# Wider-spaced modulated tiles, and thirteen modulation vectors made in another place, in a four-layer diffusion step

## The chip, the cores and the metric

The kernel runs on one core of a Trainium2 chip. The metric is the device time of one execution in microseconds. Its engines are named as in the profile: PE (TensorE, matmuls), DVE (VectorE), ACT (ScalarE), POOL (GpSimd) and SP (SyncE, which here only issues DMAs).

## What is computed

One step of a network of four layers over 384 tokens of 1024 channels: 128 context tokens and 256 latent tokens. Every layer is a mixer and an MLP, each on a normalised and modulated copy of the residual stream:

```python
for i in range(DEPTH):                       # 4 layers: recurrent, conformer, attention, recurrent
    sh1, sc1, g1, sh2, sc2, g2 = _adaln(cond, w_mod[i], b_mod[i])   # silu(cond) @ w + b, in 6 parts
    h = _rmsnorm(x) * (1 + sc1) + sh1
    x = x + g1 * mixer(h)
    h = _rmsnorm(x) * (1 + sc2) + sh2
    x = x + g2 * (jnp.square(jax.nn.relu(h @ w1)) @ w2)             # 1024 -> 4096 -> 1024
```

All of it is in fp32. The mixers are a bidirectional gated linear recurrence (layers 0 and 3), a gated convolution of width 31 (layer 1), and neighbourhood attention over a grid (layer 2).

## The kernel before

**Products.** Channels lie on the 128 partitions, tokens in the free dimension, so the stream x is eight tiles of 128 x 384. An fp32 product is made of three matmuls in a faster 32-bit format (`mm3`): both operands are split into a rounded part and the rest, and PE adds up hi x hi, hi x lo and lo x hi. Weights come in chunks of 1 MB ("raw", two buffers, on SP's queue); ACT writes the rounded part (whi, L212) and DVE the rest (wlo, L213), five buffers of 128 x 1024 each, so that weights are split well ahead of their use. All matmuls are issued at L125; the profile tells them apart by their output's name: rec, gbr, lo (recurrent layer), pw, cps (conformer), qk, v, s, pt, wo (attention), f and o (MLP). An MLP runs in two halves; in each, eight f products make 16 hidden tiles of 128 x 384 (hh and hl), and eight o products of 48 matmuls each bring them back to the residual tiles.

**The modulated copy.** `htile` (L397) gives the moving operands of f, qk, pw, rec and gbr: eight pairs of tiles, hhi and hlo, of 128 x 386, 384 tokens and two columns for the shift. The first 96 matmuls of a layer or MLP after the first stream all 386 columns of a copy not yet normalised (`Norm.start`), and the norm is applied to their result; the rest stream the 384 columns of the normalised one. Before the norm is known PE issues 24 of them, then the matmuls of the norm's total (n_1p, at `MID`). The norm's sum (n_1s) is closed on DVE after the last residual.

**Modulation vectors.** There are 4 x 6 x 8 = 192 of them, each made from 512 KB of weights, in a fixed order. `pe_mod` makes them on PE in batches of two or more (loads pmw or pmwl; 32 small matmuls into pmp for two vectors, then two matmuls with `sel` and an addition on DVE, L292). `dve_mod` (L312) makes one on DVE: a load dmw on SP's queue, two passes over it (mjunk, L325, 128 x 1024) and an addition (L328). Where each is made is written down by hand: calls `mods(n)` in the recurrent layer (PE), a call in the conformer with buffers of its own ("pm", two of them), one entry of `ATTMODS` for each pair of heads in attention, and `MLPMODS`, a number after each of the eight f or o products of a half. `need` makes at once what a layer asks for and is not there.

**Around the conformer's convolution.** Six of the eight channel tiles are convolved on PE (cps): POOL writes the padded tile to memory (zd) and reads it back in shifted windows (z, four loads), SP loads the diagonal weights (dg). Later, SP loads pmwl2 to pmwl5 for six vectors that are made on PE while PE would stand idle; two of them use the "pm" buffers, which the call `dve_mod(2, cp)` has used before, and two the z buffers.

**Order.** A scheduler places each engine's instructions by its own costs, within what buffers and dependences allow; an engine then works through its list in order, and so does SP with its loads.

Of the kernel before, what the change touches and what calls it, by code (L numbers as in the profile page):

```python
# [8 lines left out]
F32R = mybir.dt.float32r  # L9
# [5 lines left out]
P = 128  # L15
D = 1024
KT = D // P
DEPTH = 4
SEQ = 128
LAT = 256  # L20
N = SEQ + LAT
# [16 lines left out]
GW = 64  # L38
WR = 8
WC = 16  # L40

SH1, SC1, G1, SH2, SC2, G2 = range(6)

# [17 lines left out]
def weight_plan():  # L61
    plan = []
    for l in range(DEPTH):
# [11 lines left out]
        for half in range(2):  # L75
# [14 lines left out]
WARM0, WARM1, WARM2 = 20, 8, 4  # L90
RECLAG, PRE1 = 2, 8
WARM3 = (6, 6)
MLPMODS = {(False, 0, 1): (0, 1, 2, 1, 2, 1, 2, 1), (False, 0, 2): (2, 2, 2, 1, 2, 2, 2, 1),
           (False, 1, 1): (2, 2, 2, 1, 2, 2, 2, 1), (False, 1, 2): (0, 0, 0, 0, 0, 0, 0, 0),
           (True, 0, 1): (0, 1, 1, 1, 1, 2, 2, 0), (True, 0, 2): (0,) * 8,
           (True, 1, 1): (0,) * 8, (True, 1, 2): (0,) * 8}
ATTMODS = (0, 1, 1, 1, 1, 1, 1, 1)
VALMODS = 0
PTB, BTB = 3, 3
NMOD = DEPTH * 6 * KT  # L100
# [13 lines left out]
def trunk(ctx, tc, wst, wmod, vecs, condr, xin, kcT, vcache, rpbt, diag, ident_in,  # L114
          y_out, st_out, k_out, v_out):
    nc = tc.nc
# [3 lines left out]
    act = ctx.enter_context(tc.tile_pool(name="act", bufs=1))  # L120
# [14 lines left out]
    def tmp(name, dt=F32):  # L135
        return tp.tile([P, 400], dt, tag="t", name=name, bufs=7)
# [86 lines left out]
    def chunk(*key):  # L223
        i = state["w"]
        assert plan[i] == key, (plan[i], key)
        state["w"] = i + 1
        ensure(i + 2)
        return loaded[i]
# [3 lines left out]
    def mod_tile(l):  # L232
        if l not in modv:
            modv[l] = cst.tile([P, 6, KT, 2], F32, name=f"modv{l}")
        return modv[l]
# [6 lines left out]
    def next_mod(form):  # L242
        i = len(MODS)
        if i >= NMOD:
            return None
        MODS.append((form,) + order[i])
        return i, order[i]
# [64 lines left out]
    def dve_mod(n, pool=None):  # L312
        for _ in range(n):
            nx = next_mod("dve")
            if nx is None:
                return
            i, (l, m, c) = nx
            if pool:
                w = pool.tile([P, D], F32, tag="pm", name=f"dmw{i}", bufs=2)
            else:  # L320
                w = wp.tile([P, D], F32, tag="dmw", name=f"dmw{i}", bufs=3)
            nc.sync.dma_start(w, wmod[i])
            for s in range(2):
                tc.keep_in_program_order(
                    nc.vector.scalar_tensor_tensor(mjunk, w, 0.5, condb[:, s], op0=ALU.mult, op1=ALU.mult,  # L325
                                                   accum_out=mod_tile(l)[:, c, m, s:s + 1]))
            dst = mod_tile(l)[:, c, m, :]
            nc.vector.tensor_tensor(dst, dst, bmod[:, l, c, m, :], op=ALU.add)  # L328
# [66 lines left out]
            return r  # L395

    def htile(name):  # L397
        return (act.tile([P, N + 2], F32R, tag="hhi", name=name + "h", bufs=KT),
                act.tile([P, N + 2], F32R, tag="hlo", name=name + "l", bufs=KT))

    def split(src, hi, lo):
        nc.scalar.activation(hi, src, AF.Copy)
# [174 lines left out]
    def lru(l, j, nrm):  # L577
        with tc.tile_pool(name=f"lru{l}", bufs=1) as lp:
# [9 lines left out]
            def conv(b, i, ps, c=None):  # L588
                t = 2 * b + i
                r = recs[t % 2]  # L590
                for s, xa, xb in SEG:
                    o = 1 + 2 * s
                    if c is None:
                        nc.scalar.activation(r[:, xa + o:xb + o], ps[:, xa:xb], AF.Copy)
                    else:
                        nc.scalar.activation(r[:, xa + o:xb + o], ps[:, xa:xb], AF.Identity, bias=c[:, s:s + 1])
                if b not in xfs:
                    xfs[b] = lp.tile([P, 2, LG], F32, tag="xf", name=f"xf{l}{b}", bufs=2)
                xf = xfs[b][:, i]
                nc.vector.tensor_scalar(xf, r[:, 0:LG], lcw[:, j, t, 0:1], lcb[:, j, t:t + 1],  # L600
                                        op0=ALU.mult, op1=ALU.add)
                for k in range(1, 4):
                    nc.vector.scalar_tensor_tensor(xf, r[:, k:k + LG], lcw[:, j, t, k:k + 1], xf,  # L603
                                                   op0=ALU.mult, op1=ALU.add)
# [67 lines left out]
            def outs(b):  # L672
                if b < 3:
                    w_ = lp.tile([P, 1024], F32R, tag="graw", name=f"yh{l}{b}", bufs=3)
                else:
                    w_ = lp.tile([P, 4 * LG], F32R, tag="a", name=f"yh{l}{b}")
                if b:
                    lo = lp.tile([P, 2, N], F32R, tag="gl", name=f"yl{l}{b}", bufs=4)
                else:
                    lo = lp.tile([P, 2, LG], F32R, tag="xf", name=f"yl{l}{b}", bufs=2)[:, :, :N]  # L680
                for i in range(2):
                    y.append(split(gls[b][:, i], w_[:, i * N:i * N + N], lo[:, i]))

            def mods(n, pe=0):
                if l == 0:
                    dve_mod(n)
                    pe_mod(pe)

            y = []
            if l == 0:  # L690
                h = []
# [36 lines left out]
            else:  # L728
                h = nrm.start([chunk("rec", j, b) for b in range(2)], f"rec{l}_0_",
                              lambda i, t, c: conv(i // 2, i % 2, t, c))  # L730
            gbr(0)
            mods(1)
            q = gates(0)
# [21 lines left out]
            gbr(3)  # L755
            combine(3, q3)
            outs(3)
            mods(0, 4)
            nc.sync.dma_start(st_out[j], nst)
            mv = need(l, G1)  # L760
            nc.vector.tensor_scalar_mul(mv[:, G1], mv[:, G1], 0.5)
            return out_proj(l, "lout", j, y, f"lo{l}")

    def mlp(l, nrm):
        last = l == DEPTH - 1
        with tc.tile_pool(name=f"mlp{l}", bufs=1) as mp:
            for half in range(2):
                hid = []

                def act_(i, ps, c=None):  # L770
                    r = tmp(f"r{l}{half}{len(hid)}")[:, :N]
                    s = tmp(f"s{l}{half}{len(hid)}")[:, :N]
                    hh = mp.tile([P, N], F32R, tag="hh", name=f"hh{l}{half}{len(hid)}", bufs=16)
                    hl = mp.tile([P, N], F32R, tag="hl", name=f"hl{l}{half}{len(hid)}", bufs=16)
                    if c is None:
                        nc.scalar.activation(r, ps[:, :N], AF.Relu)  # L776
                    else:
                        for s_, a, b in SEG:
                            nc.scalar.activation(r[:, a:b], ps[:, a:b], AF.Relu, bias=c[:, s_:s_ + 1])
                    nc.scalar.activation(hh, r, AF.Square)  # L780
                    nc.scalar.activation(s, r, AF.Square)  # L781
                    nc.vector.tensor_tensor(hl, s, hh.bitcast(F32), op=ALU.subtract)  # L782
                    hid.append((hh, hl))

                i = 0
                while i < 8:
                    if half == 0 and i == 0:
                        h = nrm.start([chunk("ff1", l, 0), chunk("ff1", l, 1)], f"f{l}0_", act_)
                        i = 2
                    else:  # L790
                        lin([chunk("ff1", l, half * 8 + i)], h, f"f{l}{half}{i}_", act_)
                        i += 1
                    dve_mod(MLPMODS[last, half, 1][i - 1])
                mv = need(l, G2)
                if half == 1:
                    nx = Norm(l + 1, SC1, SH1)
                for m in range(KT):
                    hi, lo = chunk("ff2", l, half * 8 + m)
                    ps = mm_tile(f"o{l}{half}{m}")[:, :N]
                    for k in range(16):  # L800
                        o = (k % 8) * P
                        mm3(ps, hi[k // 8][:, o:o + P], lo[k // 8][:, o:o + P], hid[k], k == 0, k == 15)
                    residual(m, ps, G2, mv)
                    if half == 1:
                        nx.add(m)
                    dve_mod(MLPMODS[last, half, 2][m])
        return nx

    hb1 = cst.tile([P, 2 * KT], F32, name="hb1")
# [8 lines left out]
    def conformer(l, j, nrm):  # L818
        mv = need(l, G1)
        with (tc.tile_pool(name=f"cf{l}", bufs=1) as cp,  # L820
# [93 lines left out]
            def shift():  # L914
# [3 lines left out]
                for m in first:  # L918
# [3 lines left out]
            h = nrm.start([chunk("pw1", j, m) for m in range(2)], f"pw{l}0_",  # L922
                          lambda i, t, c: keep.__setitem__(i, (t, c)))
# [14 lines left out]
            conv_pe(3)  # L938
            pwin(6)
            pwin(7)  # L940
            dve_mod(2, cp)
            conv_pe(4)
            shift()
            conv_pe(5)
# [18 lines left out]
            m = KT - 1  # L963
# [62 lines left out]
    def attention(l, j, nrm):  # L1026
        with tc.tile_pool(name=f"na{l}", bufs=1) as ap:
# [184 lines left out]
            both(values(0), None)  # L1212
            dve_mod(ATTMODS[0])
            both(attend(0), values(1))
            for pr in range(1, KT):
                dve_mod(ATTMODS[pr])
                both(attend(pr), qk(pr + 1) if pr + 1 < KT else wo_first())
# [25 lines left out]
def lay_out(i):  # L1243
# [75 lines left out]
    for cq in range(GW):  # L1319
        c0 = min(max(cq - WC // 2, 0), GW - WC)  # L1320
        for rq in range(4):
            bt[:, rq, cq, :, c0:c0 + WC] = rpb[:, WR - 1 - rq:WR + 3 - rq, c0 - cq + WC - 1:c0 - cq + 2 * WC - 1]
    bt = bt.reshape(NH, 2, P, LAT)
# [46 lines left out]
```

## Time and profile before

| | |
|---|---|
| median of 3 runs | 1767.76 us (1767.61 to 1771.6) |
| profiled execution | 1769.54 us, span 1767.8 us, mean granted clock of PE 0.994 |
| layer 0 with its MLP | to 460.8 us |
| layer 1 with its MLP | to 887.3 us |
| layer 2 with its MLP | to 1340.9 us |
| layer 3 with its MLP, final norm | to the end |
| modulation vectors | 42 on PE, 150 on DVE |

In the lines below, a row of groups has line, engine, operation, out<-in, shape and count, then busy time in us and mean ns of one, then the engine's idle time ahead of them and what ended it. A row of the chain has start, length and work. A row of the windows has for each engine its busy time, then PE's granted clock, the share of time that the DMA engines were busy, and GB/s. A row of waits has the waiting line, what it waited for, us in total, times, and the longest.

### The profile page before, as it was taken

Reading aid. Unit: us, or ns where it says so; the run is one execution under the profiler, and the core shown is the slowest. Engines: PE = TensorE matmul, PEld = TensorE weight load, DVE = VectorE, ACT = ScalarE, POOL = GpSimd, SP = SyncE. Lnnn points to the kernel's source line nnn. Section 1 sums busy time; section 2 is a strip of 40 time slices with the busy share of each in tenths; the row PEclk is TensorE's granted clock in tenths of the full one; section 3 lists DMA queues with packets and bytes.
Section 4 is the critical chain, followed back from the end, with each engine's and each line's share of the span. In section 5 each row is a group of like instructions: output and inputs, shape, how many; then the busy total and the mean of one; then the engine's idle time right before and its main releaser. Section 6 shows DMA issues by size and latency. Waiting matters only on the chain.

```text
span 1767.8 us, 27418 instructions
## 1 busy us (share of the span) xinstructions
PE 1733.9 (98%) x10510; PEld 1633.5 (92%) x10510; DVE 1394.3 (79%) x2773; ACT 943.9 (53%) x1699; POOL 21.6 (1%) x46
## 2 busy tenths in 40 slices
PE   8999999999998999999999999999999999999997
PEld 7778999999984999999987889999999789999997
DVE  5998999895787889988576778998998979953443
ACT  4876662453632774255355556624545976733531
POOL 0000000000021000000000000000000000000000
PEclk9999999999999999999999999999999999999999
DMA  9666467674376247766345534676664413543341
GB/s 387 233 215 214 136 229 243 239 240 141 122 229 193 63 153 260 242 237 226 120 173 171 168 109 143 227 250 238 230 242 136 134 70 120 202 143 119 119 136 44
DMA packets 66996, 322.43 MB, mean 182 GB/s; under 512 B 7952, under 2 KB 12176, under 8 KB 43696
## 3 DMA queue, kind: packets, MB, share of 16 engines
q1 hardware_dynamic: 64944, 314.11, 51.5%
q0 software_dynamic: 1920, 6.57, 1.5%
q8 instruction: 82, 1.34, 0.3%
q14 instruction: 50, 0.41, 0.1%
HBM read 316.69 MB, written 3.96 MB: 181 GB/s over the span
## 4 chain that ended last, share of the span: by engine, by line
PE 85%; DVE 9%; ACT 4%; DMA 2%; issue 1%; POOL 0%; SPq 0%; DVEq 0%; ACTq 0%
PE f L125 30%; PE o L125 30%; PE pw L125 4%; PE qk L125 4%; PE lo L125 3%; PE p L125 2%; PE wo L125 2%; PE v L125 2%; PE cps L125 2%; PE rec L125 2%; DVE wlo L213 1%; DVE mjunk L325 1%; PE po L125 1%; DVE xf L603 1%; DVE tr L645 1%
## 5 line engine op out<-in xcount | busy, mean ns | idle before, releaser
L212 ACT ACTIVATE whi<-raw 128x1024 fp32r<-128x1024 f32 x360 | 378.3, 1058 | 553.6 <-PE o L125 333.1
L213 DVE TENSOR_TENSOR wlo<-raw,whi 128x1024 fp32r<-128x1024 f32 x360 | 438.1, 1222 | 170.3 <-ACT whi L212 169.9
L325 DVE SCALAR_TENSOR_TENSOR mjunk<-dmw,condb 128x1024 bf16<-128x1024 f32 x300 | 365.8, 1219 | 1.3
L125 PE MATMUL o<-hl,whi 128*128 128x384 f32 x1024 | 343.0, 335 | 0.0
L125 PE MATMUL o<-hh,wlo 128*128 128x384 f32 x1024 | 343.0, 335 | 0.0
L125 PE MATMUL o<-hh,whi 128*128 128x384 f32 x1024 | 343.0, 335 | 0.0
L125 PEld LDWEIGHTS o<-hh,whi 128*128 128x128 f32 x1024 | 192.2, 188 | 0.0
L125 PEld LDWEIGHTS o<-hh,wlo 128*128 128x128 f32 x1024 | 192.2, 188 | 0.0
L125 PEld LDWEIGHTS o<-hl,whi 128*128 128x128 f32 x1024 | 192.2, 188 | 0.0
L496 DVE SCALAR_TENSOR_TENSOR x<-o,modv,x 128x128 f32<-128x128 f32 (+1 forms) x128 | 47.5, 413 | 87.3 <-PE o L125 87.3
L125 PE MATMUL g<-xf,graw 128*128 128x386 f32 x256 | 85.7, 490 | 1.6 <-DVE gl L661 1.6
L782 DVE TENSOR_TENSOR hl<-s,hh 128x384 fp32r<-128x384 f32 x128 | 71.1, 556 | 11.1 <-ACT s L781 6.6
L125 PEld LDWEIGHTS g<-xf,graw 128*128 128x128 f32 x256 | 47.9, 189 | 34.2 <-DVE gl L661 2.2
L780 ACT ACTIVATE hh<-r 128x384 fp32r<-128x384 f32 x128 | 67.1, 524 | 3.4
L781 ACT ACTIVATE s<-r 128x384 f32<-128x384 f32 x128 | 65.1, 509 | 0.0
L776 ACT ACTIVATE r<-f 128x384 f32<-128x384 f32 x112 | 53.2, 475 | 10.8 <-PE f L125 10.8
L125 PE MATMUL lo<-yh,wlo 128*128 128x384 f32 x128 | 43.4, 339 | 1.3 <-DVE wlo L213 1.3
L125 PE MATMUL lo<-yh,whi 128*128 128x384 f32 x128 | 43.3, 340 | 0.0
L125 PE MATMUL cps<-z,dg 128*32 128x399 f32 (+2 forms) x448 | 34.8, 466 | 8.5 <-DMA z<-zd 8.5
L125 PE MATMUL lo<-yl,whi 128*128 128x384 f32 x128 | 43.0, 336 | 0.0
L125 PEld LDWEIGHTS cps<-z,dg 128*32 128x32 f32 x448 | 14.4, 114 | 28.1 <-issue 23.9
L892 DVE SCALAR_TENSOR_TENSOR zt<-zp,vec,zt 128x399 f32<-128x399 f32 x58 | 36.6, 632 | 1.2
(1521 smaller groups left out, 4043.9 us busy)
## 6 DMA issues: line engine op xcount, KB each, us to landing
raw<-wst SPq DMA_DIRECT2D x180, 1024.0 KB, 5.0
dmw<-wmod SPq DMA_DIRECT2D x150, 512.0 KB, 4.1
pmw<-wmod SPq DMA_DIRECT2D x38, 512.0 KB, 6.2
graw<-wst SPq DMA_DIRECT2D x16, 512.0 KB, 5.5
bt<-rpbt SPq DMA_DIRECT2D x16, 384.0 KB, 3.9
z<-zd POOLq DMA_DIRECT2D x24, 213.5 KB, 7.5
dg<-diag SPq DMA_DIRECT2D x6, 512.0 KB, 5.0
pmwl<-wmod SPq DMA_DIRECT2D x4, 512.0 KB, 6.9
```

Of the source, the lines that this page charges most:

```text
L125: i = nc.tensor.matmul(*a, **kw)
L212: nc.scalar.activation(hi, raw[:, s], AF.Copy)
L213: nc.vector.tensor_tensor(lo, raw[:, s], hi.bitcast(F32), op=ALU.subtract)
L325: nc.vector.scalar_tensor_tensor(mjunk, w, 0.5, condb[:, s], op0=ALU.mult, op1=ALU.mult, accum_out=mod_tile(l)[:, c, m, s:s + 1]))
L496: nc.vector.scalar_tensor_tensor(x[m][:, xa:xb], ps[:, a:b], mv[:, g, m, s:s + 1], x[m][:, xa:xb], op0=ALU.mult, op1=ALU.add)
L603: nc.vector.scalar_tensor_tensor(xf, r[:, k:k + LG], lcw[:, j, t, k:k + 1], xf, op0=ALU.mult, op1=ALU.add)
L645: nc.vector.tensor_tensor_scan(tr[:, 2 + mt, ::-1], a[:, 2 + mt, ::-1], ti[:, 2 + mt, ::-1], h0v[:, j, 1, t:t + 1], op0=ALU.mult, op1=ALU.add)
L776: nc.scalar.activation(r, ps[:, :N], AF.Relu)
L780: nc.scalar.activation(hh, r, AF.Square)
L781: nc.scalar.activation(s, r, AF.Square)
L782: nc.vector.tensor_tensor(hl, s, hh.bitcast(F32), op=ALU.subtract)
L892: nc.vector.scalar_tensor_tensor(t, z[:, k:k + CG], dww[:, m, k:k + 1], t, op0=ALU.mult, op1=ALU.add)
```

## The change

Three things change. (1) h tiles are allocated 512 columns wide and cut to 386, so they lie 2048 bytes apart; their tags are now hh and hl of the same pool. In the built programs they were 1568 bytes apart before, at changing offsets within 512 bytes, and all begin at the same offset after. The hidden tiles are 1536 bytes, as they were. The room comes from the descriptor scratch of POOL's DMAs, halved to 8192 bytes. (2) Four vectors on PE at the end of layer 0, two on DVE in the conformer and seven on DVE in attention are no longer made there. (3) The table for the MLPs is by layer and half: for layer 0 eleven vectors after the second half's o products, for layer 1 eight of them there and eight instead of ten after its first f products, for layer 2 seven instead of ten after its first f products and fourteen after its second half's o products. There, eleven were made before already: ten that layer 3 would ask for had been placed that early by the scheduler. Layer 3's MLP is left with four of its eight. In all 38 vectors are made on PE and 154 on DVE.

```diff
+HP = 512
-MLPMODS = {(False, 0, 1): (0, 1, 2, 1, 2, 1, 2, 1), (False, 0, 2): (2, 2, 2, 1, 2, 2, 2, 1),
-           (False, 1, 1): (2, 2, 2, 1, 2, 2, 2, 1), (False, 1, 2): (0, 0, 0, 0, 0, 0, 0, 0),
...
-ATTMODS = (0, 1, 1, 1, 1, 1, 1, 1)
+LIGHT, HEAVY, NONE = (0, 1, 2, 1, 2, 1, 2, 1), (2, 2, 2, 1, 2, 2, 2, 1), (0,) * 8
+EVEN = (1,) * 8
+MLPMODS = {0: (LIGHT, HEAVY, HEAVY, (2, 1, 2, 1, 2, 1, 2, 0)),
+           1: ((0, 1, 1, 1, 2, 1, 2, 0), HEAVY, HEAVY, EVEN),
+           2: (EVEN, HEAVY, HEAVY, HEAVY),
+           3: ((0, 1, 1, 1, 1, 2, 2, 0), NONE, NONE, NONE)}
+ATTMODS = (0,) * 8
...
     def htile(name):
-        return (act.tile([P, N + 2], F32R, tag="hhi", name=name + "h", bufs=KT),
-                act.tile([P, N + 2], F32R, tag="hlo", name=name + "l", bufs=KT))
+        return tuple(act.tile([P, HP], F32R, tag=f"h{q}", name=name + q, bufs=KT)[:, :N + 2] for q in "hl")
...
             outs(3)
-            mods(0, 4)
...
-                    dve_mod(MLPMODS[last, half, 1][i - 1])
+                    dve_mod(MLPMODS[l][2 * half][i - 1])
...
-                    dve_mod(MLPMODS[last, half, 2][m])
+                    dve_mod(MLPMODS[l][2 * half + 1][m])
...
             pwin(7)
-            dve_mod(2, cp)
             conv_pe(4)
...
-    nc = bacc.Bacc("TRN2", target_bir_lowering=False, num_devices=1)
+    nc = bacc.Bacc("TRN2", target_bir_lowering=False, num_devices=1, dynamic_dma_scratch_size=8192)
```

The change moves rows on three engines at the places that matter below. PE at the end of layer 0, before (pmp: vectors; lo: the output product, whi12 and wlo12 its first chunk, whi13 and wlo13 the next):

```order
600 L125 MATMUL lo000_1724<-yh01_1435,wlo12_0_1579 128x384
601 L125 MATMUL pmp42_1675<-pmw42_1676,condp_99 32x128 x2
602 L125 MATMUL lo001_1725<-yh01_1435,whi12_1_1582 128x384
603 L125 MATMUL lo001_1725<-yl01_1436,whi12_1_1582 128x384
604 L125 MATMUL lo001_1725<-yh01_1435,wlo12_1_1583 128x384
605 L125 MATMUL lo002_1726<-yh00_1429,whi13_0_1706 128x384
606 L125 MATMUL lo002_1726<-yl00_1430,whi13_0_1706 128x384
607 L125 MATMUL lo002_1726<-yh00_1429,wlo13_0_1707 128x384
608 L125 MATMUL lo003_1727<-yh00_1429,whi13_1_1710 128x384
609 L125 MATMUL lo003_1727<-yl00_1430,whi13_1_1710 128x384
610 L125 MATMUL pmp42_1675<-pmw43_1678,condp_99 32x128 x2
```

and after:

```order
592 L129 MATMUL lo001_1675<-yh01_1435,whi12_1_1582 128x384
593 L129 MATMUL lo001_1675<-yl01_1436,whi12_1_1582 128x384
594 L129 MATMUL lo001_1675<-yh01_1435,wlo12_1_1583 128x384
595 L129 MATMUL lo002_1676<-yh00_1429,whi13_0_1656 128x384
596 L129 MATMUL lo002_1676<-yl00_1430,whi13_0_1656 128x384
597 L129 MATMUL lo003_1677<-yh00_1429,whi13_1_1660 128x384
598 L129 MATMUL lo002_1676<-yh00_1429,wlo13_0_1657 128x384
599 L129 MATMUL lo003_1677<-yl00_1430,whi13_1_1660 128x384
600 L129 MATMUL lo002_1676<-yh00_1429,whi13_0_1656 128x384
```

The pmp rows are gone, and chunk 13 comes 24 rows after the last gbr; its wlo is asked for in row 598.

SP's queue in the conformer, before (raw: weights; dg: diagonals; pmwl: the late vectors' weights):

```order
166 L206 DMA raw58_5937<-wst 128x2048
167 L206 DMA raw59_6099<-wst 128x2048
168 L161 DMA pmwl2_5666<-wmod 128x1024
169 L854 DMA dg17_5487<-diag 128x1024
170 L161 DMA pmwl3_5668<-wmod 128x1024
171 L161 DMA pmwl4_5670<-wmod 128x1024
172 L322 DMA dmw90_6534<-wmod 128x1024
173 L161 DMA pmwl5_5672<-wmod 128x1024
```

and after:

```order
163 L165 DMA pmwl2_5661<-wmod 128x1024
164 L165 DMA pmwl3_5663<-wmod 128x1024
165 L210 DMA raw52_5013<-wst 128x2048
166 L210 DMA raw53_5088<-wst 128x2048
167 L210 DMA raw54_5163<-wst 128x2048
168 L210 DMA raw55_5344<-wst 128x2048
169 L210 DMA raw56_5419<-wst 128x2048
170 L210 DMA raw57_5922<-wst 128x2048
...
174 L210 DMA raw59_6094<-wst 128x2048
175 L855 DMA dg17_5492<-diag 128x1024
176 L165 DMA pmwl4_5665<-wmod 128x1024
177 L326 DMA dmw95_6529<-wmod 128x1024
```

pmwl2 and pmwl3 have moved ahead of raw52; behind raw59 only dg17, pmwl4 and a dmw are left.

DVE at the end of layer 2, before (x7: the last residual; n3_1s: the sum for layer 3's norm; dmw: a vector's weights):

```order
1913 L213 TENSOR_TENSOR wlo141_1_13569<-raw141_13562,whi141_1_13568 128x1024
1914 L496 SCALAR_TENSOR_TENSOR x7_86<-o217_13486,modv2_6870,x7_86 128x128
1915 L496 SCALAR_TENSOR_TENSOR x7_86<-o217_13486,modv2_6870,x7_86 128x256
1916 L213 TENSOR_TENSOR wlo142_0_13575<-raw142_13572,whi142_0_13574 128x1024
1917 L372 TENSOR_TENSOR n3_1s_13539<-n3_1a_13106,n3_1q7_13537 128x384
```

and after:

```order
1922 L217 TENSOR_TENSOR wlo141_0_13605<-raw141_13602,whi141_0_13604 128x1024
1923 L332 TENSOR_TENSOR modv3_11621<-modv3_11621,vec_70 128x2
1924 L329 SCALAR_TENSOR_TENSOR mjunk_108,modv3_11621<-dmw187_13588,condb_107 128x1024
1925 L217 TENSOR_TENSOR wlo141_1_13609<-raw141_13602,whi141_1_13608 128x1024
1926 L499 SCALAR_TENSOR_TENSOR x7_86<-o217_13521,modv2_6612,x7_86 128x128
1927 L499 SCALAR_TENSOR_TENSOR x7_86<-o217_13521,modv2_6612,x7_86 128x256
1928 L329 SCALAR_TENSOR_TENSOR mjunk_108,modv3_11621<-dmw187_13588,condb_107 128x1024
1929 L376 TENSOR_TENSOR n3_1s_13574<-n3_1a_13086,n3_1q7_13572 128x384
```

Vectors 185 to 187 now stand between the residuals of the last two products and the sum, where none stood.

More of the change, by code (lines that the diff above doesn't have):

```diff
@@ L92 @@
 WARM3 = (6, 6)
-MLPMODS = {(False, 0, 1): (0, 1, 2, 1, 2, 1, 2, 1), (False, 0, 2): (2, 2, 2, 1, 2, 2, 2, 1),
-           (False, 1, 1): (2, 2, 2, 1, 2, 2, 2, 1), (False, 1, 2): (0, 0, 0, 0, 0, 0, 0, 0),
-           (True, 0, 1): (0, 1, 1, 1, 1, 2, 2, 0), (True, 0, 2): (0,) * 8,
-           (True, 1, 1): (0,) * 8, (True, 1, 2): (0,) * 8}
-ATTMODS = (0, 1, 1, 1, 1, 1, 1, 1)
+LIGHT, HEAVY, NONE = (0, 1, 2, 1, 2, 1, 2, 1), (2, 2, 2, 1, 2, 2, 2, 1), (0,) * 8
[5 more added lines that the diff above has]
+ATTMODS = (0,) * 8
 VALMODS = 0
@@ L764, in mlp @@
     def mlp(l, nrm):
-        last = l == DEPTH - 1
         with tc.tile_pool(name=f"mlp{l}", bufs=1) as mp:
```

## The prediction

> **What bounds the kernel now.** I read the page's busy times first, then the chain of work that ended last, then the windows stage by stage, then inside the stages that are not full the waits.
>
> ```profile
> PE 1733.9 (98%) x10510; PEld 1633.5 (92%) x10510; DVE 1394.3 (79%) x2773; ACT 943.9 (53%) x1699; POOL 21.6 (1%) x46
> PE 85%; DVE 9%; ACT 4%; DMA 2%; issue 1%; POOL 0%; SPq 0%; DVEq 0%; ACTq 0%
> core 0: us, PE busy (x) PEld busy (x) DVE busy (x) ACT busy (x) POOL busy (x), PEclk, DMA share, GB/s
> 193.20:460.80 267.60, 267.60 (x1539) 267.60 (x1539) 219.21 (x393) 128.96 (x216) 0.00 (x0) 1.00 0.58 201
> 460.80:619.60 158.80, 147.39 (x1153) 124.10 (x1152) 133.38 (x284) 80.87 (x161) 19.85 (x38) 0.97 0.51 155
> 921.20:1047.20 126.00, 125.62 (x773) 100.34 (x772) 91.35 (x319) 71.98 (x188) 0.00 (x0) 1.00 0.46 153
> ```
>
> PE is busy for 98% and makes 85% of the chain. The MLP after the first recurrent layer (193.2 to 460.8) has not a gap on PE, the attention pairs (921 to 1047) lack 0.4 us, and the conformer (460.8 to 619.6) stands 11.4 us idle. So time is won by fewer or quicker matmuls anywhere, or by ending the conformer's idle time; moving DVE work wins nothing unless PE waits for DVE.
>
> Inside that MLP the chain falls into its four products ("f" into the hidden tiles, "o" out of them):
>
> ```profile
> 193.19 4.24 PE f L125 x24
> 197.78 62.93 PE f L125 x360
> 260.70 66.56 PE o L125 x384
> 327.26 66.99 PE f L125 x384
> 394.25 66.56 PE o L125 x384
> ```
>
> Same count and width, yet o takes 66.56 / 384 = 173.3 ns a matmul twice over, and f 66.99 / 384 = 174.45, or 62.93 / 360 = 174.8 where part of it streams the 386-column tiles. Both have a whi and a wlo chunk as weights; only the moving tile differs.
>
> **Part A, the 2048-byte tiles.** The f, qk, pw, rec and gbr products stream h tiles: 386 x 4 = 1544 bytes, laid out so that neighbours begin at different offsets within 512 bytes. The o products stream hidden tiles of 1536 bytes, three times 512, so all of those begin at the same offset; these are the flat 173.3. The change gives h tiles one common offset too. If that is what f lacks, f goes to 173.3: the second half gains 66.99 - 66.56 = 0.43, the first 62.93 - 360 x 0.1733 = 0.53, and its first 24 gain 4.24 - 4.16 = 0.08. That is 1.04 for an MLP and 4.2 for four. The layers begin with 96 matmuls on the 386-column tiles, here the attention's:
>
> ```profile
> 887.27 4.23 PE qk L125 x24
> 891.85 12.79 PE qk L125 x72
> ```
>
> These are 176.3 and 177.6 ns, 0.07 + 0.31 = 0.38 over the o rate, 1.1 for three layers that start so. Two columns in 384 are worth 0.9 ns by the same rate (an estimate), which over 7 x 96 matmuls is 0.6 that stays. With 0.3 for the rest of pw, qk, rec and gbr, where PE is not always the limit: 4.2 + 1.1 - 0.6 + 0.3 = **-5.0**. Bounds: -5.8 if all of it goes; 0 if the offset is not the cause; above 0 if 2048 bytes is worse than 1568 (both are among the rivals).
>
> [...]
>
> **Part B, four vectors leave the end of the first recurrent layer.** Each batch of two is 32 matmuls of weights, 2 small ones, and an addition on DVE.
>
> ```profile
> L125 PE MATMUL pmp<-pmw,condp 128*32 128x128 f32 x64 | 2.6, 276 | 0.4 <-DVE yl L403 0.4
> L125 PE MATMUL pmp<-pmw,condp x64: 269/273/297, 155.8 to 164.1; 128*32 128x128 f32 x64
> 159.66 1.13 DVE wlo L213
> ...
> 161.37 0.41 PE pmp L125 x4
> 161.78 1.60 PE lo L125 x8
> 163.38 1.00 PE pmp L125 x28
> ...
> 165.11 0.12 PE pmp L125 x2
> ```
>
> The 64 matmuls take 2.6 us and have 0.4 of idle time before them; a pair of small ones takes 0.12, so two pairs 0.24. All of it lies on PE, which from their start at 155.8 on has work without them: 24 lo matmuls of a chunk split before, 4.2 us at some 174 ns. What is late next: at 160.0 PE comes to chunk 13, three matmuls later (160.5) it needs that chunk's wlo, which begins at 159.66 and ends at 160.8: 0.3 late. After it the reordered rows put other lo products ahead of what DVE still owes. So 2.6 + 0.24 + 0.4 - 0.3 = **-2.9**, from -1.5 (a wait as long as the first batch) to -3.2. The four 512 KB loads leave SP's queue there; nothing waits for them.
>
> **Part C, two DVE vectors leave the conformer.** Their arithmetic is free: DVE has idle time behind it. Their loads hold the two "pm" buffers, and SP must wait for these before it can issue the next loads.
>
> ```profile
> 547.77 5.54 PE cps L125 x60
> 553.32 2.68 issue
> 556.00 1.64 POOL z L851 x3
> 557.63 9.50 DMA z<-zd
> 567.38 5.17 PE cps L125 x64
> 547.70:560.50 12.80, 10.85 (x129) 3.97 (x128) 12.62 (x27) 4.27 (x8) 4.34 (x8) 1.00 1.00 330
> 560.50:567.30 6.80, 0.29 (x4) 0.00 (x0) 2.10 (x5) 1.15 (x3) 0.00 (x0) 0.73 0.94 230
> 567.30:572.60 5.30, 5.22 (x65) 2.84 (x66) 0.00 (x0) 0.00 (x0) 0.00 (x0) 0.70 0.04 16
> PE cps L125 <- DMA z<-zd: 8.5, 2, 6.6
> SPq L161 <- DVE modv L328: 7.8, 2, 5.9
> pmwl<-wmod SPq DMA_DIRECT2D x4, 512.0 KB, 6.9
> z<-zd POOLq DMA_DIRECT2D x8, 213.5 KB, 6.6
> ```
>
> The last channel tile's window z is asked for from 556.0 on and is there at 557.63 + 9.50 = 567.13; PE waits 6.6 us for it, with the DMA engines full (shares 1.00 and 0.94). Among what they carry are two pmwl loads that SP could issue only once the two vectors were added up (7.8 us of waits), and with them the dg load queued behind the first. Without the vectors the order of SP's queue has both ahead of seven raw loads, about where the two dmw loads stood, so 1.05 MB leaves the crowd: 1.05 MB at 330 GB/s is 3.2 us, at 230 GB/s 4.6. I take 4.2, nearer the second since that is the rate while PE waits; z's own four pieces, 0.85 MB, need 3.7 us at it, so it can't land before 559.7. Then PE's wait is some 2.5 us.
>
> The convolution after the wait runs at a granted clock of 0.70: 5.22 us there are 3.65 at 1.00, so up to 1.6 more if the shorter wait leaves the clock alone. I take half. Sum: -4.2 - 0.8 = **-5.0**; from -1.5, if the crowd is shared out otherwise, to -7. [...]
>
> **Part D, seven vectors leave attention.** PE waits there only once:
>
> ```profile
> PE pt L1143 <- DVE pe L1135: 0.4, 1, 0.4
> ```
>
> DVE has 91.35 busy of 126, so the seven hide: **-0.4**, from 0 to -1 (the loads also leave SP's queue).
>
> **Part E, where the thirteen go.** They go into MLPs, where DVE has room or not:
>
> ```profile
> 394.20:460.80 66.60, 66.60 (x386) 66.60 (x385) 36.72 (x67) 26.69 (x48) 0.00 (x0) 1.00 0.43 146
> 327.30:394.20 66.90, 66.90 (x385) 66.90 (x384) 60.44 (x101) 36.68 (x63) 0.00 (x0) 1.00 0.69 234
> 1274.40:1340.90 66.50, 66.50 (x385) 66.50 (x385) 59.49 (x117) 27.00 (x48) 0.00 (x0) 1.00 0.66 224
> 1328.50:1340.90 12.40, 12.40 (x73) 12.40 (x72) 5.77 (x11) 4.32 (x8) 0.00 (x0) 1.00 0.44 138
> L325 DVE SCALAR_TENSOR_TENSOR mjunk<-dmw,condb x300: 1212/1218/1228, 64.5 to 1555.1; 128x1024 bf16<-128x1024 f32 x150
> ```
>
> A vector is two mjunk of 1.22 and an addition, 2.5 us. Layer 0's second o product goes from 36.7 (with the one vector that falls there) to 36.7 + 10 x 2.5 = 62 of 66.6, as full as the f product of 60.4 that has no gap; its 5 MB of loads go where the DMA share is 0.43. Layer 1's goes to 55: nothing. Layer 2's already holds 11, since the ones that the last layer will ask for are pulled forward; with 14 it needs 59.5 + 7.6 = 67 of 66.5, and the last 12.4 us, where DVE has 6.6 of idle time, now hold three more. In the new order one mjunk (1.22) stands between the last residual and the norm's sum, and one vector and a half before that residual. PE has 24 rec matmuls (4.2 us) before it asks for the norm. I price this at **+1.5**, one mjunk and a little; from 0 to +3 (the whole overload).
>
> **Sum:** -5.0 - 2.9 - 5.0 - 0.4 + 1.5 = -11.8. The profiled execution took 1769.54 (span 1767.8), so its like would take 1757.7; it lies 1.8 above the median of 1767.76, from which the forecast is 1756.0. The smaller scratch for POOL's descriptors and the last MLP's four vectors instead of eight I cost at nothing: POOL is busy 1%, and that MLP is full on PE without them.
>
> **The rivals.** (i) *The spacing does nothing*, so the change doesn't do what it seems to: f stays 174.45 against o's 173.3. For it: the hidden tiles differ from h in more than their offsets. Then -6.8: 1761.0. (ii) *z is no earlier*: the dmw and raw loads behind move up and fill the same 10 us, DMA full to 567. For it: the share of 1.00. Against it: SP's next loads wait for buffers that are freed later. Then -11.8 + 5.0: 1761.0. With (i) as well, 1766.0. (iii) *Slower*: tiles a round 2048 bytes apart get in each other's way. It would strike some 4,600 matmuls (3,072 f, the rest pw, qk, rec, gbr); parts B to E give -6.8, so it decides from (6.8 + 5.3) / 4600 = 2.6 ns each, to 176 ns; at 4 ns, +18.4 - 6.8 = +11.6: 1779.4. Against it: hidden tiles a multiple of 512 apart are the quickest of all.
>
> **How the numbers follow.** The forecast gets 0.60, (i) 0.17, (ii) 0.13, both 0.04, (iii) 0.05, 0.01 anything else. All the best ends together are -5.8 - 3.2 - 7 - 1 + 0 = -17.0: 1750.8. The upper end takes in (i) and (ii) alone, 1761.0 and 2 us of unknown costs: 1763.0. What a measurement can tell from no change is 0.3%, 5.3 us: faster means below 1762.5. The forecast is wholly there, (i) and (ii) for four fifths (0.24 of 0.30): 0.84; within 0.3%: 0.11; slower: 0.05.
>
> **What would show it.** Right: f pieces of 384 at 66.6, no pmp between 155 and 166, z for the last tile landing near 563 and a cps wait under 3 us with a higher clock behind it, and a rec wait for the norm of 1 to 2 us at the third MLP's end. Wrong: f still at 66.99 (A), cps still waiting 6 us (C), a wait of lo for wlo of over 1 us (B), or PE waiting for wlo inside an o product (E).

## The result and the profile after

The changed kernel takes 1757.98 us (median of 4 runs, 1757.02 to 1760.51), the kernel before 1768.18 beside it (median of 4, 1767.61 to 1771.6). The ratio is 0.9945, 95% interval 0.9932 to 0.9957: faster by 0.55%, where 1756.0 had been forecast. The profiled execution of the changed kernel took 1757.44, span 1755.7, so 12.1 us less of span than the profiled one of before. Executions of one kernel differ by some us (25 of the kernel before, run side by side, by 8.4), and two single executions of over 4900 us, one of the kernel before and one of `more` below, count in no ratio.

The times between the first matmuls of products that follow each other show where it went (us, one profiled execution each; the kernel's start, up to the last gbr of layer 0, gives the 0.2 that is missing from the sum):

| stretch | forecast | before | after | difference |
|---|---|---|---|---|
| end of the last gbr of layer 0 to first f | -2.9 (B) | 37.14 | 33.74 | -3.40 |
| four MLPs, the last with the final norm | -4.2 (A) | 1083.08 | 1081.03 | -2.05 |
| conformer: first pw to first f | -5.0 (C), A's share | 158.76 | 154.31 | -4.45 |
| attention: first qk to first f | -0.4 (D), A's share | 186.06 | 184.04 | -2.02 |
| last recurrent layer: first rec to first f | +1.5 (E), A's share | 146.83 | 146.89 | +0.06 |

The chain through layer 0's MLP, after; it answers to the f and o pieces of before:

```profile
189.55 5.30 PE f L129 x30
195.79 61.42 PE f L129 x352
257.21 66.56 PE o L129 x384
323.77 66.57 PE f L129 x384
390.34 66.56 PE o L129 x384
456.90 4.24 PE pw L129 x24
```

f in the second half is now as quick as o, 66.57 against 66.99. The trace also shows how: measured from one start to the next in this second half, a matmul took 171.7 to 179.4 ns before, depending on the h tile that it streams, and takes 173.0 to 173.5 now, whichever it is. But the products on 386 columns are hardly quicker: 5.30 / 30 = 176.7 ns and 4.24 / 24 = 176.7, against 176.7 (4.24 / 24) for f's first 24 before.

The conformer's chain and PE's waits there, after:

```profile
543.52 4.98 issue
548.50 1.64 POOL z L852 x3
550.13 8.51 DMA z<-zd
558.64 0.25 issue
558.88 5.32 PE cps L129 x64
PE cps L129 <- DMA z<-zd: 4.5, 1, 4.5
558.80:564.20 5.40, 5.32 (x65) 2.86 (x65) 0.00 (x0) 0.00 (x0) 0.00 (x0) 0.68 0.26 104
```

PE waits 4.5 us instead of 8.5, but the last z still takes 8.51 us to land (9.50 before), and the clock behind it is 0.68 still. Counted from the first pw, the last z is issued 3.6 us earlier than before (93.4 instead of 97.0) and lands 4.6 us earlier: most of the gain was there before it was issued.

Layer 2's second o product and what follows, windows of the changed kernel:

```profile
1262.40:1328.90 66.50, 66.50 (x386) 66.50 (x385) 66.36 (x134) 27.44 (x47) 0.00 (x0) 1.00 0.72 244
1328.90:1345.40 16.50, 16.50 (x95) 16.41 (x94) 16.39 (x42) 10.31 (x20) 0.79 (x2) 1.00 0.53 199
```

DVE is as full as was worked out (66.36 of 66.5), and PE has no gap.

### The profile page after: what moved, and what is told of

Its sections match the earlier page's. It is cut to its first block, busy times and chain, and to the rows that moved or that the text cites. A ratio compares the mean times of both kernels' runs of the same rounds, so it can differ in the third digit from the quotient of the medians.

```text
span 1755.7 us, 27298 instructions
## 1 busy us (share of the span) xinstructions
PE 1725.0 (98%) x10442; PEld 1626.0 (93%) x10442; DVE 1404.6 (80%) x2791; ACT 946.3 (54%) x1697; POOL 21.6 (1%) x46
## 3 DMA queue, kind: packets, MB, share of 16 engines
q8 instruction: 82, 1.34, 0.3%
## 4 chain that ended last, share of the span: by engine, by line
PE 77%; DVE 15%; ACT 4%; issue 2%; DMA 1%; SPq 0%; POOL 0%; DVEq 0%; ACTq 0%
PE f L129 29%; PE o L129 27%; PE pw L129 4%; PE lo L129 3%; DVE mjunk L329 3%; PE qk L129 3%; DVE wlo L217 2%; PE p L129 2%; PE wo L129 2%; PE v L129 2%; DVE xf L606 1%; PE cps L129 1%; PE s L129 1%; PE po L129 1%; DVE tr L648 1%
## 5 line engine op out<-in xcount | busy, mean ns | idle before, releaser
L329 DVE SCALAR_TENSOR_TENSOR mjunk<-dmw,condb 128x1024 bf16<-128x1024 f32 x308 | 375.7, 1220 | 1.5
L129 PEld LDWEIGHTS g<-xf,graw 128*128 128x128 f32 x256 | 47.9, 190 | 34.4 <-DVE gl L664 2.5
L129 PEld LDWEIGHTS cps<-z,dg 128*32 128x32 f32 x448 | 14.6, 114 | 23.8 <-issue 22.4
```

The lines of the kernel that those rows point to most:

```text
L129: i = nc.tensor.matmul(*a, **kw)
```

## The experiments

Two theories stand at the start for the conformer: that of the prediction, that the two vectors' loads crowd the last z; and a race of two transfers much earlier. The second comes from both traces: the changed kernel is ahead in the conformer long before the loads that were thought to matter. Counted from the first pw, the conformer's fifth raw load is issued at 41.7 us instead of 45.6, its eighth and last at 80.2 instead of 83.3. Ahead of the fifth, about 37 us after the first pw, DVE, which convolves two channel tiles there, waits, 4.7 us before and 0.8 after. It waits for ACT's whi, and that for a raw load issued 31 us after the first pw, as POOL issues the first four z loads. That load took 9.7 us before and 5.8 after.

### layout: the tiles alone

```diff
+HP = 512
...
+        return tuple(act.tile([P, HP], F32R, tag=f"h{q}", name=name + q, bufs=KT)[:, :N + 2] for q in "hl")
...
+    nc = bacc.Bacc("TRN2", target_bir_lowering=False, num_devices=1, dynamic_dma_scratch_size=8192)
```

> The tiles 2048 bytes apart and the smaller descriptor scratch alone; all vectors where they were. Theory of the offsets: f pieces of 384 go from 66.99 to 66.57 as in the changed kernel, products on 386 columns stay near 177 ns, about -2.5 us in all, and attention's pairs stay at 14.76 us. Rival for attention: the 2 us gained there come from the tiles' places in memory, then a pair takes 14.43 us and the sum is -4.5. For the conformer: if its gain comes from the two vectors' loads, it keeps its 123.2 us from the first pw to the first p; if it comes from which of two transfers gets ahead early in the convolution (DVE's 4.65 us wait about 37 us after the first pw), it may show 123.2 or about 119 here too, with the wait or without it.

1764.75 us (median of 12, before 1768.1), ratio 0.999, interval 0.9971 to 1.001: the total can't be told from no change, but the stages can. Its MLPs with the final norm take 1080.4, 2.7 us less than before, with f as in the changed kernel:

```profile
326.84 66.57 PE f L126 x384
393.41 66.56 PE o L126 x384
459.97 4.24 PE pw L126 x24
```

Attention's pairs stay at 14.76 us. The conformer takes 156.0 from pw to f, and DVE's early wait is there, 3.4 us. So the tiles are worth 2.7 us in the MLPs, and attention's gain is not theirs.

### vectors: the thirteen vectors alone

```diff
-        return tuple(act.tile([P, HP], F32R, tag=f"h{q}", name=name + q, bufs=KT)[:, :N + 2] for q in "hl")
+        return (act.tile([P, N + 2], F32R, tag="hhi", name=name + "h", bufs=KT),
+                act.tile([P, N + 2], F32R, tag="hlo", name=name + "l", bufs=KT))
```

(against the changed kernel, and the descriptor scratch as before)

> The thirteen vectors moved as in the changed kernel, tiles and descriptor scratch as before. If the parts add up: 10.2 less the 2.5 of the tiles, so -7.7, with the recurrent layer's end -3 us, attention -2, the conformer -4.4. If the conformer's gain hangs on the early race of two transfers and not on the vectors, the conformer may keep its 123.2 us, and the sum is about -4.

1763.33 (median of 6, 1757.01 to 1764.7; two of the six took 1757.0 and 1757.5), ratio 0.9961, interval 0.9946 to 0.9977; -4.8 against -7.7 expected. In the profiled execution, of 1763.72, the recurrent layer's end (33.71), the conformer (154.2) and attention's pairs (14.42) are as expected. What is missing lies in two other stretches. In the kernel's start the last gbr ends 1.5 us later than before (157.4 against 155.9), and that end differs from profile to profile (154.6 to 158.4 over all kernels here). Attention as a whole takes 185.56, 0.5 less than before instead of the 2 expected: from its first qk to its first po it takes 1.7 us longer than before. Why these two differ stays open.

### rec4 and conf2: four vectors, two vectors

```diff
-            mods(0, 4)
```
```diff
-            dve_mod(2, cp)
```

(each against the kernel before; the vectors go after layer 0's second o products)

> Only the four vectors at the end of the first recurrent layer leave; they are made after its MLP's second output products on DVE. From the last gbr to the first f: 37.2 us before, 33.9 after the whole change. Theory: 34.2 here and -3 us in all, nothing lost in the MLP. Rival: the 0.3 us beyond the pmp matmuls are the tiles', then 34.3 to 34.5. The conformer is untouched: if its first 45 us show DVE's 4.65 us wait here, it is as before; if they don't, the race theory holds and the sum is near -7.

> Only the conformer's two vectors leave; they are made after the first MLP's second output products. Theory of the prediction: two loads of 512 KB no longer crowd the last z, which lands some 4 us earlier after its issue or the same 9.5 us after an issue that is no earlier; -4 to -5 us with DVE's early wait of 4.65 us still there. Race theory: if that early wait (37 us after the first pw) stays, the last z comes no more than 1.5 us earlier and the gain is under 2; if it goes, about -4.4 as in the changed kernel.

rec4: 1757.19 (median of 6), ratio 0.9943, interval 0.9929 to 0.9956: the four vectors alone give as much as the whole change, and more than the 7 us that were expected at best. The recurrent layer's end takes 33.71, so -3.4; and the conformer, in which nothing is changed, takes 149.2 instead of 158.8, with no early wait of DVE and the last z in 6.49 us, though the two loads that were thought to crowd it are there:

```profile
549.11 6.49 DMA z<-zd
555.85 3.66 PE cps L126 x64
PE cps L126 <- DMA z<-zd: 0.8, 1, 0.8
```

Behind a wait of 0.8 us the 64 matmuls take 3.66 instead of 5.17 us, close to the 3.65 that the prediction worked out for a clock of 1.00; so the clock was kept there (an estimate from these times).

conf2: 1767.22 (median of 12), ratio 0.9992, interval 0.9984 to 1.0001: nothing. Its conformer takes 156.9, 1.8 less, with an early wait that is 1.0 shorter (3.6). The last z is issued as late as before and takes 7.0 us instead of 9.5, so the two vectors' loads may count for something there; but the 4 to 5 us of the prediction's theory don't come.

### What starts the race: before_fill and rec4_fill

One row stands in only one of the traces at that moment. Here are the 12.1 us from 30.9 after the first pw on (DMA queues, issues and DVE's wait), before and then after:

```profile
q8 instruction: 1, 0.02, 0.8%
raw<-wst SPq DMA_DIRECT2D x2, 1024.0 KB, 9.9
z<-zd POOLq DMA_DIRECT2D x4, 213.5 KB, 10.3
DVE wlo L213 <- ACT whi L212: 4.7, 1, 4.7
```

```profile
raw<-wst SPq DMA_DIRECT2D x3, 1024.0 KB, 5.8
z<-zd POOLq DMA_DIRECT2D x4, 213.5 KB, 7.5
DVE wlo L217 <- ACT whi L216: 0.8, 1, 0.8
```

In before, a load of instructions, 16 KB, falls on the first microsecond of the raw load (32.2 after the first pw); in the changed kernel there is none, it came at 23.7. In the trace of before, from 204.1 to 470.8 us, where PE does nothing but matmuls of some 174 ns, such loads come 17.9 to 26.1 us apart, 22.2 on average, one for 128 matmuls; in the whole execution there are 82 of them for 10510 matmuls, again 128. So it looks like PE's own instruction stream, which is inferred from these counts. The 68 matmuls of the four vectors fewer should then move it by 68 x 0.174 = 11.8 us (an estimate from these figures), so that the one at 10.2 comes at 22; measured 23.7. That can be tried: add matmuls to the kernel before, or give rec4 as many as it lost.

```diff
+        if l == 0:
+            warm(24, "fill", mm_tile)     # before_fill, on the kernel before; 34 in rec4_fill, on rec4
         with tc.tile_pool(name=f"mlp{l}", bufs=1) as mp:
```

> The kernel before with 24 such matmuls (48 in PE's stream, about 2.7 us) ahead of the first MLP, and nothing else. Theory of the instruction fetch: the fetch at 32.2 us after the first pw moves to about 24, DVE's early wait goes from 4.65 us to under 1, and the conformer from 123 to 113 to 119 us: although work is added, the kernel is faster by 1.5 to 7 us (1761 to 1766.5). Rival: the conformer stays at 121 to 123, and the kernel is 2.7 us slower, 1771.

> rec4 with 34 idle matmuls on a scratch tile (two passes each, 68 in PE's stream, about 4 us) put ahead of the first MLP, so that PE's instruction stream is as long as before again. Theory of the instruction fetch: the 16 KB fetch that falls 23.5 us after the conformer's first pw in rec4 falls at about 32 again, as in before, layout and conf2, inside the raw load that is issued at 31; DVE's wait of 3.4 to 4.7 us returns and the conformer takes 118 to 123 us instead of 113.7. With the matmuls' 4 us, 1764 to 1770 in all. Rival, that it is the vectors and their loads at the recurrent layer's end: the conformer stays at 113.7 and the sum is 1761.

before_fill, then rec4_fill, the same 12.1 us:

```profile
raw<-wst SPq DMA_DIRECT2D x3, 1024.0 KB, 5.6
z<-zd POOLq DMA_DIRECT2D x4, 213.5 KB, 7.0
DVE wlo L213 <- ACT whi L212: 0.5, 1, 0.5
```

```profile
q8 instruction: 1, 0.02, 0.8%
raw<-wst SPq DMA_DIRECT2D x2, 1024.0 KB, 9.1
z<-zd POOLq DMA_DIRECT2D x4, 213.5 KB, 9.4
DVE wlo L214 <- ACT whi L213: 2.8, 1, 2.8
```

Idle matmuls added to the kernel before take the early wait away: its conformer goes from 158.8 to 148.3 us, the shortest of all. In rec4, as many as it had lost bring the wait back, at 2.8 us a little under the 3.4 to 4.7 expected, and its conformer goes from 149.2 to 156.0. The totals are 1766.8 (median of 10, ratio 0.9998, interval 0.9987 to 1.0009) and 1772.1 (ratio 1.003, interval 1.0017 to 1.0044): the fill cost 5.5 and 7.5 us at the recurrent layer's end where 2.7 and 4 had been put down, so before_fill missed its range of 1761 to 1766.5 by a little, rec4_fill its 1764 to 1770 by 2.1, and the gain shows in the stage and not in the sum. All the kernels, in the order of the load of instructions after the first pw (us):

| kernel | instructions at | raw load takes | conformer, pw to f |
|---|---|---|---|
| ln44 (below) | 22.1 | 6.0 | 154.7 |
| rec4 | 23.5 | 5.3 | 149.2 |
| conf_back (below) | 23.6 | 5.8 | 154.3 |
| after | 23.7 | 5.8 | 154.3 |
| vectors | 23.7 | 5.5 | 154.2 |
| hp448 (below) | 23.7 | 5.8 | 154.5 |
| before_fill | 23.8 | 5.6 | 148.3 |
| more, second run (below) | 24.2 | 5.5 | 154.5 |
| before | 32.2 | 9.7 | 158.8 |
| rec4_fill | 32.3 | 7.9 | 156.0 |
| layout | 32.4 | 8.4 | 156.0 |
| conf2 | 32.7 | 8.7 | 156.9 |
| att7 (below) | 34.4 | 7.6 | 157.1 |

The last raw load of the conformer goes out 79.7 to 80.5 us after the first pw in the eight kernels above and 81.2 to 83.3 in the five below. So the early wait itself is worth about 3 us against before; the rest of before_fill's 10.5 arises after that load. How a load of 16 KB, 0.8% of the DMA engines' time in these 12.1 us, can cost a raw load 2 to 4 us is not shown.

### conf_back and ln44: what holds the last z

Among the kernels without the early wait there are still two sorts, 148 to 149 and 154 to 155.

```diff
+            dve_mod(2, cp)
             conv_pe(4)
```
```diff
-LNMODS, LNPRE, LNMB = 6, 6, 4
+LNMODS, LNPRE, LNMB = 4, 4, 4
```

(each against the changed kernel; ln44 with `LNFIN = (2,)` and its two vectors after layer 0's second o products)

> The changed kernel with the conformer's two vectors put back. In rec4, which still has them, the conformer takes 113.7 us from the first pw to the first p, and 118.8 in the changed kernel: without the vectors the dg load goes out with the last zd and holds it up (zd 7.0 us and z 8.4 there, 5.9 and 6.5 in rec4). So if that is the cause: 113 to 115 here, -4 to -5 against the changed kernel, about 1753 us. The prediction's theory, that the vectors' loads crowd the last z: +4 to +5 against the changed kernel, 1762.

> The changed kernel with four vectors instead of six made on PE late in the conformer; the other two go after the first MLP's second output products (thirteen there). SP then issues one load of 512 KB (a dmw) where it issued two (pmwl4 and the dmw) some 92.3 us after the first pw, among the four z loads of the last tile. Where both come before the last z (after, conf_back, att7, layout), that z takes 8.5 to 9.7 us to land; where they come after it (rec4, before_fill), 6.5 to 7.4. Theory: those two loads set the last z; half of them gone, it takes 7 to 8 us, the conformer 115 to 117.5 us and the kernel 1755. Rival: dg, issued with the last zd, sets it; then it stays at 118.8 and the kernel at 1757 to 1758.

conf_back: 1757.25 (median of 6, 1753.95 to 1762.56), the changed kernel's time; conformer 154.3, not 149. Putting the vectors back neither costs 4 us (the prediction's theory) nor wins 4 (that of the dg load), so neither expectation came true. Its last zd is as quick as in rec4 (5.9 us), but its last z is issued at 92.7, after or with SP's two loads at 92.3 and 92.7, and takes 9.1 us; in rec4 it is issued at 92.0, ahead of them at 92.6 and 93.0, and takes 6.5. ln44, with one load there instead of two: 1758.97 (median of 5), conformer 154.7, last z 8.3 us where 7 to 8 was expected. So neither load settles it, and conf2, whose last z follows SP's loads and still takes 7.0, speaks against their order as the whole cause. (Of the kernels named in the expectation, att7's last z takes 10.5 us, outside the 8.5 to 9.7 given.) What makes the last z 6.5 or 9 us stays open.

### att7: attention alone

```diff
-ATTMODS = (0, 1, 1, 1, 1, 1, 1, 1)
+ATTMODS = (0,) * 8
```

(against the kernel before, with one vector after each of the second MLP's second o products)

> Only attention's vectors leave; they are made after the second MLP's second output products. Attention's pairs take 14.76 us in every kernel that has the vectors there (before, layout, rec4, conf2) and 14.42 in the two that don't (after, vectors), whatever the tiles. So here 14.42, six pairs and a half less, -2 us for attention as a whole and -2 in all. The prediction's step said -0.4, from the waits alone. Rival: the pairs gain only together with what else the change moves, then 14.76 and nothing. PE's instruction stream is as long as before up to the conformer, so the conformer stays at 121 to 123 us with DVE's early wait of 3.4 to 4.7 us.

1765.45 (median of 12), ratio 0.999, interval 0.998 to 1.0; pairs of 14.40 us, attention as a whole 184.81 instead of 186.06. So the pairs gain 0.35 each, from the vectors, as in the changed kernel: 2.5 us from the first po to the last group of them. But the whole gains only 1.25 of the 2 expected, since the stretch from the first qk to the first po takes 1.0 us longer; in the changed kernel that stretch takes 0.2 longer, in vectors 1.7. The chain shows what the pairs gain by. Here is the start of a pair, before and after (po: probabilities x values of a pair's two heads; pt: a transpose), and behind each the group of all these po products in attention:

```profile
966.07 0.36 PE po L125 x2
966.43 0.26 PE pt L1143
966.69 0.36 PE po L125 x2
L125 PE MATMUL po<-pT,vl 128*64 128x128 f32 x32 | 5.7, 298 | 0.0
```

```profile
956.62 0.37 PE po L129 x4
956.99 0.48 PE pt L1143 x3
L129 PE MATMUL po<-pT,vl 128*64 128x128 f32 x32 | 3.5, 298 | 0.0
```

A head's product is 64 columns wide on PE (128*64 in the groups). Back to back the two heads' take 0.37 us together; with a transpose between them, 0.36 each. Without the vectors on DVE the scheduler's order has them back to back: 0.35 us a pair, with PE full in both (busy 125.62 of 126 us before, 123.98 of 124 after). The 32 small po products take 3.5 us in att7 and vectors too, and 5.7 in layout.

### hp448: another distance

```diff
-HP = 512
+HP = 448
```

> The changed kernel with the modulated tiles 1792 bytes apart instead of 2048, so that neighbours begin 256 bytes apart within 512. Theory of the common offset: f on these tiles goes back from 66.57 for 384 to about 67, 1.7 to 2.5 us in all. Rival, that any distance which is a multiple of 256 does as well: 66.57 and no difference.

1760.42 (median of 5, 1758.06 to 1764.23), ratio 0.9957, interval 0.9943 to 0.9971. f is as quick as at 2048 bytes:

```profile
323.27 66.57 PE f L129 x384
389.84 66.56 PE o L129 x384
```

Tiles 256 bytes apart in their offset do as well, so "one common offset" asks for too much: 1792 and 2048 bytes, both multiples of 256, gave 66.57 each, and a smaller step was not tried. The total is 2.4 us above the changed kernel's median, but the executions spread over 6 us and the intervals overlap.

### more: sixteen vectors in layer 2

```diff
-           2: (EVEN, HEAVY, HEAVY, HEAVY),
+           2: (EVEN, HEAVY, HEAVY, (2,) * 8),
```

> The changed kernel with sixteen instead of fourteen vectors after the third MLP's second output products; the last MLP makes two instead of four. DVE has 66.36 us of work in those 66.5 in the changed kernel, and PE waits for nothing there. By the prediction's step a vector more is 2.5 us late at the boundary: now 69 to 71 us in 66.5, so rec waits for the norm and the third MLP with the start of the recurrent layer is 2.5 to 4 us longer. Rival: DVE's work ahead of the norm's sum doesn't grow, since the vectors behind it are put after the sum or the split of weights is pushed back: under 1 us.

> The kernel with sixteen vectors there once more, since its profiled execution ran at a granted clock that can't be compared. Its median was 1766.1, 8 us over the changed kernel. Theory of the overload: the third MLP's second half and the start of the last recurrent layer hold those 8 us, with PE waiting for DVE (the norm's split, or a split of weights). Rival: they lie elsewhere, in the conformer, whose time hangs on transfers, or in the last MLP.

1766.11 (median of 10), ratio 0.9984, interval 0.9975 to 0.9993, and again 1764.87 (median of 8), ratio 0.9982, interval 0.9971 to 0.9994: 7 to 8 us over the changed kernel. The last recurrent layer takes 152.7 us instead of 146.9, 5.8 more; its conformer is the changed kernel's (154.5), attention 1.4 longer, and the third MLP itself takes the same 266.9. Here are windows of the layer's first 71 us in the second run, the same stretch of the changed kernel beside the second (1345.40), and a wait:

```profile
1330.60:1347.10 16.50, 16.50 (x94) 16.17 (x93) 16.42 (x38) 6.68 (x13) 0.79 (x2) 1.00 0.64 232
1347.10:1401.70 54.60, 52.03 (x230) 40.44 (x229) 51.16 (x94) 47.93 (x83) 0.00 (x0) 1.00 0.40 131
1345.40:1400.00 54.60, 54.60 (x240) 42.72 (x239) 50.23 (x89) 49.66 (x83) 0.00 (x0) 1.00 0.38 123
PE g L129 <- DVE xf L606: 1.1, 1, 1.1
```

So the loss comes later than at the norm, for which PE has no wait. DVE starts its last pass for a vector there 10.0 us after the first rec, instead of 2.6 in the changed kernel, and its first xf, with which the recurrence begins, comes 24.8 us after the first rec instead of 19.9. From the first rec to the first f PE stands idle for 7.9 us instead of 3.2, in several waits of the recurrence.

## Why the prediction came out right, and where it was wrong

The total, 1756.0 against 1757.98, and the sign are right; of the five terms one, B, is right in cause and near in size.

**A, the tiles, -5.0.** Cause right, size wrong: 2.7 us in layout's MLPs, 2.05 in the changed kernel's. The step that failed is the 386-column products, "0.38 over the o rate": at 176.5 to 177 ns they are at most 0.8 ns quicker than before, so those two columns cost 176.7 - 173.3 = 3.4 ns where 0.9 was worked out from the rate. Of the f products the second halves gave 0.42 each where 0.43 was forecast, the first halves of layout 0.24 on average of their 0.61. f's 66.57 at two other distances (2048 and 1792 bytes) against 66.99 at 1568 shows that the distance between tiles matters here; by what mechanism is not shown. Rival (i), that the spacing does nothing, falls, and so does (iii), that it slows the products.

**B, the recurrent layer's end, -2.9.** Right in cause: -3.4 in the whole change and in rec4, 0.2 beyond the far end of its bounds. Some 0.3 of the 0.5 that it came out larger lie in the five steps from a gbr or lo matmul to a pmp, which took 268, 174, 727 (0.4 us of it the wait), 269 and 179 ns where the median step from lo to lo took 175 (an estimate from the starts in the trace of before). The wait for chunk 13's wlo, put at 0.3, is there:

```profile
PE lo L129 <- DVE wlo L217: 0.2, 1, 0.2
```

What B did elsewhere was not foreseen: with 68 matmuls fewer the loads of instructions moved, and DVE's early wait left the conformer.

**C, the conformer, -5.0.** Right in size (-4.45), wrong in cause. The failed step is "1.05 MB leaves the crowd": without those loads the last z took 8.51 us instead of 9.50, and conf2 and conf_back show the two vectors to be worth 1.8 and 0 us. Some 3 of the 4.45 us are the early wait's, by the conformer's last raw load (issued at 80.2 instead of 83.3), which goes out ahead of those loads; that the clock would half recover did not happen (0.68 behind a wait of 4.5). Behind the wait of 4.5 us the 64 matmuls took 5.32 us, behind rec4's 0.8 us 3.66; how long a wait the clock bears is not shown.

**D, attention, -0.4.** Mis-sized: -2.0 here, -1.25 in att7 and -0.5 in vectors, of which the pairs give -2.5 each time and the stretch ahead of them takes some back. It was read from PE's waits alone. The loss was in the order of PE's own instructions, where a busy engine shows no wait.

**E, layer 2's overload, +1.5.** Wrong: 0. DVE's sum was right, but the row that was taken as added, a mjunk of 1.22 between the last residual and the norm's sum, stands where the order of before has a wlo (wlo142_0) of the same length, which now follows the sum. So the sum starts 2.6 us after the first rec instead of 2.3, and PE has no wait there. Sixteen vectors are too many: they cost 5.8 us in the last recurrent layer.

So the total is right partly by luck: A and C were put some 3.5 us too high, and B, D and E together as much too low. Of the rivals, (ii) was nearest to the truth about the loads, and missed that the conformer would gain all the same.

## What to carry to other kernels

When a stage gains, look for the first moment at which the two traces part, not for the wait that was longest; here that moment lay over 50 us ahead of the longest wait, and experiments that leave the stage untouched (rec4, the fills) were what showed it. A full engine can still lose time by its order: compare the order of its instructions, not only its waits (a pair of heads took 14.76 us in one order and 14.42 in the other, with PE full in both). Before an added instruction is counted as an added delay, see what left the same place: the mjunk of 1.22 us, which stood where a wlo of 1.22 had stood, made the norm's sum 0.3 us later.

## What the hardware showed that was not expected

Loads of instructions stand beside data in the profile's DMA tables (queue q8, 82 of them with 1.34 MB in the page of before, so 16 KB each). Where one came 32.2 to 34.4 us after the first pw, inside a raw load issued at some 31 that ran beside four z loads, the raw load took 7.6 to 9.7 us instead of 5.3 to 6.0, in five kernels against eight; adding or removing matmuls 300 us earlier moved it in and out. So a change in the number of instructions went with several us in a stage it never touched: 24 idle matmuls more, and before_fill's conformer took 148.3 us instead of 158.8. The best medians (changed kernel 1757.98, conf_back 1757.25, rec4 1757.19) can't be told apart here, and no version was found that is clearly better than the changed kernel; rec4 with the wide tiles was not run.
